# One decoder block on one core: orders of ACT's work, place of a weight load, banks and slots

## The chip, the cores and the metric

The kernel runs on 1 core of one Trainium2 chip. The metric is the device time of one execution in microseconds; the time before is the median of 3 runs.

## The reference

The block mixes 1024 tokens of width 1024 by two mixers and ends with a feed-forward layer, all in float32:

```python
u = rmsnorm(h, ln_mix);  z = u @ w_in        # columns: latents, GLA q/k/v/low rank/gate, gate_a, gate_b
y_a = mla(c_q, c_kv, k_rope, ...) @ mla_w_o  # 8 heads, causal; k_rope: one rotary key shared by the heads
y_b = gla(g_q, g_k, g_v, g_lr, ...) @ gla_w_o
#   log_a = log_sigmoid(g_lr @ w_gate2 + b_gate) / 16; chunked scan over the tokens with decay exp(cumsum(log_a))
h = h + (sigmoid(gate_a) * y_a + sigmoid(gate_b) * y_b) @ w_out
u = rmsnorm(h, ln_ffn)
h = h + (silu(u @ w_gate) * (u @ w_up)) @ w_down
out = rmsnorm(h, final_norm)
```

## The kernel before, in words

A float32 product is made of three TensorE matmuls: each operand is split into a rounded high part and a low part that holds the rest, and `mm3` (L132 to L134) adds high by high, high by low and low by high. The high part of a weight is a cast on ACT (L114, L160), the low part a subtraction on DVE or POOL (L115, L161). So each product of 128x128 by 128x512 has three matmuls, and each new weight block costs a DMA, a cast and a subtraction before them. Large products are cut into a 2x2 scheme with fewer block products (`pair`, `p_first`, `p_second` and so on), whose partial sums go through tiles `st`.

The program is written stage by stage; a scheduler then sets the order of the instructions on each engine from the written order, the dependencies and the slots of the pools. Every engine then works through its own list strictly in order, and SP issues nearly all loads and stores from one such list. Weights arrive in pool tag `wr` (4 slots of 128x1024); a load can only start when the last reader of its slot is done.

**Input (L303 to L335).** SP loads the gains `g_mix` (L92, through `gain_cols`), then four tiles of x. They are normalised (`norm_in`: square on ACT, `rx` on POOL, scaling on DVE), turned by PE into 8 PSUM banks (chunks c0 to c7, four of them with tag `ps_mm`), and each chunk is read three times: by ACT with the gain (L316, high part), by DVE (L317, low part) and by ACT again (L329, an unsplit copy `raw0`). `begin` then makes two blocks of q, from weights `wh`/`wl`. The first product writes a `ps_mm` bank, so it needs the first chunk's bank back.

**Log decay (L413 to L431).** Four half tiles go through Abs and Exp (L422, L423) and, in a second loop, through Ln (L430). The sums over the chunks follow on PE (L441).

**Gates and rotary key (L740 to L860).** Behind the scan come the latents' norms (`latents`, `token_rows`), the last two pairs of blocks of gate_b (`O_GB + 512`, `O_GB + 768`), the rotary key `krr` (L793 to L800: a load of 64x1024, a product with the table on DVE, two matmuls with `sel`), and `up_weights(1)`, which loads two 128x1024 pieces of w_ukv (L726) into `wr` and splits them (L728, L729).

**Feed-forward layer.** The second half of the tokens is turned in `second_half` (L1320 to L1347): eight transposed chunks, all in PSUM tag `B` (4 banks). Slots of 128x1024 come from pool `r4` (14).

**Down projection (L1380 to L1500).** The hidden activations come back from DRAM as `xr` (9 slots), the weights as `dr`/`y` (`load_y(c, 0)` and `load_y(c, 1)`). Loop b0 runs over 11 chunks (`chunk`: 12 matmuls, eight with the high, four with the low part of `xr`), then loop b1 with the difference of the two weight halves (L1500).

Of the kernel before, what the change touches and what calls it, by code (L numbers as in the profile page):

```python
# [10 lines left out]
F32 = mybir.dt.float32  # L11
# [9 lines left out]
P = 128  # L21
S = 1024
# [26 lines left out]
def block_kernel(ctx, tc, x, positions, ln_mix, w_in, norm_cq, w_uq, norm_ckv, w_ukv, w_oa,  # L49
# [29 lines left out]

    ident = const.tile([P, P], F32, name="ident")  # L80
# [8 lines left out]

    g_mix = gain_cols(ln_mix[0], KC, "g_mix")  # L90
# [179 lines left out]
    with ExitStack() as s1:  # L270
# [35 lines left out]
        def begin(off, out, e):  # L306
            w = wload(win[:, off:off + P], KC, P, nc.vector)
            out(e, 0, proj(w, 0), True)
            first.append((w, out, e))
# [5 lines left out]
        def turned_split(dst, ps, gc):  # L315
            nc.scalar.activation(dst[0], ps, AF.Copy, scale=gc)  # L316
            nc.vector.scalar_tensor_tensor(dst[1], ps, gc, dst[0].bitcast(F32), ALU.mult, ALU.subtract)  # L317

# [4 lines left out]
        xn = [norm_in(load_x(t)) for t in range(4)]  # L323
        for c in range(KC):
# [3 lines left out]
            turned_split(T[("B11", "B21")[j]][k], ps, gc)  # L328
            nc.scalar.activation(raw0[k][j], ps, AF.Copy, scale=gc)  # L329
        begin(O_GQ, out_q, 0)  # L330
        begin(O_GQ + P, out_q, 1)
# [83 lines left out]
    for i in range(4):  # L415
# [7 lines left out]
        nc.scalar.activation(ab, ab, AF.Exp, scale=-1.0)  # L423
# [5 lines left out]
    for ab, l in la:  # L429
        nc.scalar.activation(ab, ab, AF.Ln, bias=1.0)  # L430
# [352 lines left out]
    def q_split(c, half, cr):  # L783
# [20 lines left out]

# [48 lines left out]
    wv_h, wv_l = (t.rearrange("p (c h n) -> p c h n", c=2, h=8) for t in wtiles2())  # L853
    up_weights(1, wv_h, wv_l)
# [3 lines left out]
    p_second(w, out_gb)  # L858
    tab = [uslot(0, F32) for e in range(2)]
# [244 lines left out]
    def slot(name, dt=F32):  # L1104
        return r4.tile([P, S], dt, name=name, tag="r4", bufs=14)
# [50 lines left out]
    def transposed(xn, cc):  # L1156
        ps = pbank("B", 4)
# [162 lines left out]
    def second_half():  # L1320

        T = []
        for c in range(4):
# [6 lines left out]
            p22 = transposed(xn1, c + 4)  # L1330
# [237 lines left out]
```

## Time and profile before

| what | before |
|---|---|
| median of 3 runs | 1518.63 us (1518.12 to 1520.06) |
| the profiled execution's own time | 1514.89 us |
| its span | 1513.2 us |
| PE busy | 1456.1 us, 96% |
| DVE / ACT / POOL busy | 67% / 44% / 31% |
| mean granted clock of TensorE | 0.989 |

The profiled execution is 3.74 us below the median. Outside its span lie 1.7 us. PE is busy for 96% of the span, so about 57 us of idle PE are spread over it. A granted clock of 1.00 is 2.4 GHz, one of 0.50 is 1.2 GHz.

### The profile page before, as it was taken

Reading aid. Unit: us, or ns where it says so; the run is one execution under the profiler, and the core shown is the slowest. Engines: PE = TensorE matmul, PEld = TensorE weight load, DVE = VectorE, ACT = ScalarE, POOL = GpSimd, SP = SyncE. Lnnn points to the kernel's source line nnn. Section 1 sums busy time; section 2 is a strip of 40 time slices with the busy share of each in tenths; the row PEclk is TensorE's granted clock in tenths of the full one; section 3 lists DMA queues with packets and bytes.
Section 4 is the critical chain, followed back from the end, with each engine's and each line's share of the span. In section 5 each row is a group of like instructions: output and inputs, shape, how many; then the busy total and the mean of one; then the engine's idle time right before and its main releaser. Section 6 shows DMA issues by size and latency. Waiting matters only on the chain.

```text
span 1513.2 us, 20379 instructions
## 1 busy us (share of the span) xinstructions
PE 1456.1 (96%) x7454; PEld 1214.8 (80%) x7454; DVE 1017.8 (67%) x1459; ACT 673.3 (44%) x1329; POOL 464.0 (31%) x406
## 2 busy tenths in 40 slices
PE   6999999999979999999999899999999999899997
PEld 5789887788757888877899778888888888688886
DVE  4867886888474777574612876666666667876875
ACT  6553344644454766576302632222222223254454
POOL 1311230212102114234812455555555554100000
PEclk9999999999989999999999999999999999999999
DMA  7124234242431004258722223233223324943461
GB/s 228 46 91 151 84 104 133 63 132 92 139 105 51 9 35 139 99 168 269 263 81 84 84 71 98 97 105 105 98 98 105 101 94 166 399 131 95 135 195 56
DMA packets 123158, 181.52 MB, mean 120 GB/s; under 512 B 12897, under 2 KB 76914, under 8 KB 123058
## 3 DMA queue, kind: packets, MB, share of 16 engines
q1 hardware_dynamic: 122482, 178.38, 35.8%
q10 hardware_dynamic: 576, 1.84, 0.3%
q8 instruction: 59, 0.97, 0.3%
q14 instruction: 41, 0.34, 0.1%
HBM read 125.66 MB, written 54.53 MB: 119 GB/s over the span
## 4 chain that ended last, share of the span: by engine, by line
PE 49%; DVE 3%; DMA 1%; issue 0%; ACT 0%; POOL 0%; DVEq 0%; POOLq 0%
PE psB L133 6%; PE psB L134 6%; PE psB L132 6%; PE psA L132 4%; PE psA L134 4%; PE psD L134 4%; PE psD L132 4%; PE psD L133 4%; PE psA L133 4%; PE psy L134 1%; PE psy L132 1%; PE psy L133 1%; DMA xr<-d_a 1%; DMA dr<-in_ffn_w_down_dram 0%; DVE UT L161 0%; DMA d_h<-h 0%
## 5 line engine op out<-in xcount | busy, mean ns | idle before, releaser
L161 DVE TENSOR_TENSOR ws<-wr,ws 128x512 fp32r<-128x512 f32 x135 | 128.3, 960 | 15.5 <-ACT ws L160 14.9
L160 ACT CAST ws<-wr 128x512 fp32r<-128x512 f32 x157 | 94.2, 617 | 64.6 <-DVE wr L177 25.7
L95 POOL TENSOR_TENSOR rx<-rs_m,nhalf 128x1 f32<-128x1 f32 x24 | 14.8, 623 | 264.5 <-DVE rs_m L94 263.1
L132 PE MATMUL ps_mm<-u,ws 128*128 128x512 f32 x208 | 84.5, 407 | 10.9 <-ACT st L204 10.3
L161 POOL TENSOR_TENSOR ws<-sS,ws 128x512 fp32r<-128x512 f32 x44 | 70.7, 1616 | 67.9 <-ACT ws L160 67.9
L134 PE MATMUL ps_mm<-u,ws 128*128 128x512 f32 x208 | 83.3, 404 | 0.0
L133 PE MATMUL ps_mm<-u,ws 128*128 128x512 f32 x208 | 83.1, 399 | 0.0
L160 ACT CAST ws<-xr 128x512 fp32r<-128x512 f32 x73 | 45.2, 621 | 84.3 <-PE psB L134 39.1
L1206 ACT COPY p<-psA 128x512 f32<-128x512 f32 x22 | 12.9, 587 | 156.6 <-PE psA L134 156.6
L612 POOL TENSOR_TENSOR X<-E,gk 128x512 f32<-128x512 f32 x28 | 42.0, 1506 | 129.9 <-ACT E L610 69.7
L161 DVE TENSOR_TENSOR ws<-xr,ws 128x512 fp32r<-128x512 f32 x73 | 50.2, 688 | 37.1 <-ACT ws L160 34.5
L133 PE MATMUL psB<-UT,ws 128*128 128x512 f32 x176 | 69.8, 397 | 2.4 <-DVE UT L161 2.4
L176 DVE TENSOR_TENSOR st<-st,ps_mm 128x512 f32<-128x512 f32 x75 | 51.1, 683 | 30.9 <-PE ps_mm L134 28.8
L132 PE MATMUL psB<-UT,ws 128*128 128x512 f32 x176 | 69.8, 396 | 0.1
L132 PE MATMUL psA<-UB,ws 128*128 128x512 f32 x176 | 69.6, 396 | 0.0
L134 PE MATMUL psB<-UT,ws 128*128 128x512 f32 x176 | 69.6, 395 | 0.0
L134 PE MATMUL psA<-UB,ws 128*128 128x512 f32 x176 | 69.5, 395 | 0.0
L133 PE MATMUL psA<-UB,ws 128*128 128x512 f32 x176 | 69.3, 394 | 0.0
L935 DVE TENSOR_TENSOR ws<-pspt,ws 128x512 fp32r<-128x512 f32 (+1 forms) x80 | 49.6, 632 | 17.4 <-ACT ws L934 16.9
L916 ACT ACTIVATE u<-pss,nb 128x128 f32<-128x128 f32 (+3 forms) x64 | 47.8, 747 | 25.0 <-DVE nb L914 14.7
L160 ACT CAST ws<-sS 128x512 fp32r<-128x512 f32 x88 | 50.3, 619 | 18.1 <-DVE sS L1182 18.1
L132 PEld LDWEIGHTS ps_mm<-u,ws 128*128 128x128 f32 x208 | 39.4, 189 | 20.7 <-ACT st L204 10.8
(464 smaller groups left out, 4734.8 us busy)
## 6 DMA issues: line engine op xcount, KB each, us to landing
xr<-d_a SPq DMA_DIRECT2D x73, 256.0 KB, 2.9
wr<-in_w_in_dram SPq DMA_DIRECT2D x32, 512.0 KB, 4.1
wr<-in_ffn_w_gate_dram SPq DMA_DIRECT2D x22, 512.0 KB, 3.8
wr<-in_ffn_w_up_dram SPq DMA_DIRECT2D x22, 512.0 KB, 3.8
d_a<-p SPq DMA_DIRECT2D x20, 512.0 KB, 2.9
dr<-in_ffn_w_down_dram SPq DMA_DIRECT2D x14, 512.0 KB, 6.8
d_a<-R SPq DMA_DIRECT2D x10, 512.0 KB, 2.6
xt<-in_x_dram SPq DMA_DIRECT2D x8, 512.0 KB, 6.4
```

Of the source, the lines that this page charges most:

```text
L95: nc.gpsimd.tensor_tensor(dst, m, nhalf[:, :n], ALU.pow)
L132: nc.tensor.matmul(ps, ah, bh, start=first, stop=False, **kw)
L133: nc.tensor.matmul(ps, ah, bl, start=False, stop=False, **kw)
L134: nc.tensor.matmul(ps, al, bh, start=False, stop=last, **kw)
L160: nc.scalar.copy(dst[:, 0], src)
L161: (lo_eng or nc.gpsimd).tensor_tensor(dst[:, 1], src, dst[:, 0].bitcast(F32), ALU.subtract)
L176: plus = lambda d, x, y: nc.vector.tensor_tensor(d, x, y, ALU.add)
L612: nc.gpsimd.tensor_tensor(X, E, k, ALU.mult)
L916: nc.scalar.activation(pt[:, 0:w], ps[:, 0:w], AF.Exp, bias=bias, accum_out=sums[h // 2][:, t, e:e + 1])
L935: nc.vector.tensor_tensor(tl[:, 0:w], ps[:, 0:w], th[:, 0:w].bitcast(F32), ALU.subtract)
L1206: nc.scalar.copy(tt[:, 0:HALF], psA)
```

## The change

1. Input: `g_mix` is loaded behind the first four tiles of x. The second L316 (c1) is put behind the first chunk's copy. The low parts of the first two weights go to POOL.
2. Log decay: each Ln is put behind the last Exp that was written.
3. `O_GB + 768`'s loads and its `p_first` and `p_second` are written ahead of `krr` and of `up_weights(1)`.
4. Feed-forward layer: pool `r4` has 15 slots; the chunks `p22` of `second_half` are turned into PSUM tag `D` (2 banks).
5. Down projection: `xr` has 14 slots; `load_y(., 1)` starts at c = 8, no longer at c = 4.

`behind` adds an order on one engine, no semaphore.

```diff
@@ -77,6 +77,12 @@
     const = pool("const", side="left")
     wpool = pool("wpool", side="left")
 
+    def behind(later, first):
+
+        tc.add_manual_dep(later.ins, first.ins.name,
+                          mybir.DependencyInfo(mybir.DependencyClass.NoSync, mybir.DependencyReason.DATA),
+                          reason="issue order")
+
...
@@ -86,8 +92,6 @@
         t = const.tile([P, n], F32, name=name)
         nc.sync.dma_start(t, ap.rearrange("(c p) -> p c", p=P))
         return t
-
-    g_mix = gain_cols(ln_mix[0], KC, "g_mix")
 
     def rstd_of(dst, ssq, n, scale, epool):
         m = epool.tile([P, n], F32, name="rs_m", tag="rs_m")
@@ -303,8 +307,8 @@
                 mm3(ps, w[0][:, c, :], w[1][:, c, :], *T[f"B{j + 1}{half + 1}"][k], c == 0, c == KC - 1)
             return ps
 
-        def begin(off, out, e):
-            w = wload(win[:, off:off + P], KC, P, nc.vector)
+        def begin(off, out, e, lo_eng=nc.vector):
+            w = wload(win[:, off:off + P], KC, P, lo_eng)
             out(e, 0, proj(w, 0), True)
             first.append((w, out, e))
 
@@ -313,22 +317,28 @@
             minus(dst[1], src, dst[0].bitcast(F32))
 
         def turned_split(dst, ps, gc):
-            nc.scalar.activation(dst[0], ps, AF.Copy, scale=gc)
+            hi = nc.scalar.activation(dst[0], ps, AF.Copy, scale=gc)
             nc.vector.scalar_tensor_tensor(dst[1], ps, gc, dst[0].bitcast(F32), ALU.mult, ALU.subtract)
+            return hi
 
         out_q = store(d_q, (0, P), scale=0.125)
         out_k = store(d_k, (0, P))
 
         raw0 = [parts(v4(F32)) for c in range(4)]
-        xn = [norm_in(load_x(t)) for t in range(4)]
+        xs0 = [load_x(t) for t in range(4)]
+        g_mix = gain_cols(ln_mix[0], KC, "g_mix")
+        xn = [norm_in(xt) for xt in xs0]
+        copied = None
         for c in range(KC):
             j, k = divmod(c, 4)
             gc = g_mix[:, c:c + 1]
             ps = turned(xn, c, "mm" if c < 4 else "g")
-            turned_split(T[("B11", "B21")[j]][k], ps, gc)
-            nc.scalar.activation(raw0[k][j], ps, AF.Copy, scale=gc)
-        begin(O_GQ, out_q, 0)
-        begin(O_GQ + P, out_q, 1)
+            hi = turned_split(T[("B11", "B21")[j]][k], ps, gc)
+            if c == 1:
+                behind(hi, copied)
+            copied = nc.scalar.activation(raw0[k][j], ps, AF.Copy, scale=gc)
+        begin(O_GQ, out_q, 0, nc.gpsimd)
+        begin(O_GQ + P, out_q, 1, nc.gpsimd)
         xn = [norm_in(load_x(t)) for t in range(4, 8)]
         begin(O_GK, out_k, 0)
         t12, t4 = [], []
@@ -420,14 +430,14 @@
                              wg2[0:17, :], start=True, stop=True)
         ab = g.tile([P, HALF], F32, name="lab", tag=("E", "gk")[i // 2], bufs=2)
         nc.scalar.activation(ab, ps, AF.Abs)
-        nc.scalar.activation(ab, ab, AF.Exp, scale=-1.0)
+        ex = nc.scalar.activation(ab, ab, AF.Exp, scale=-1.0)
         if i % 2 == 0:
             la2 = g.tile([P, S], F32, name="la", tag="A", bufs=2)
         l = la2[:, (i % 2) * HALF:(i % 2 + 1) * HALF]
         nc.vector.tensor_scalar(l, ps, 0.0, None, ALU.min)
         la.append((ab, l))
     for ab, l in la:
-        nc.scalar.activation(ab, ab, AF.Ln, bias=1.0)
+        behind(nc.scalar.activation(ab, ab, AF.Ln, bias=1.0), ex)
         nc.vector.tensor_tensor(l, l, ab, ALU.subtract)
     def gb_tile():
         return g.tile([P, HALF], F32, name="gb", tag="gb", bufs=2)
@@ -789,19 +799,6 @@
     sc_q = small.tile([P, NT], F32, name="sc_q", tag="sc_q", bufs=1)
     nc.vector.tensor_scalar(sc_q, rs_q, 96.0 ** -0.5, None, ALU.mult)
     rq_ps = token_rows(sc_q)
-
-    krr = wraw(1024)[0:64]
-    nc.sync.dma_start(krr, d_c[640:704, :])
-    nc.vector.tensor_tensor(krr, krr, rot[0:64], ALU.mult)
-    nc.gpsimd.tensor_tensor(sel, ident[0:64, 0:32].unsqueeze(1).broadcast_to([64, 4, 32]),
-                            ident[0:64, 32:64].unsqueeze(1).broadcast_to([64, 4, 32]), ALU.add)
-    kr_ps = []
-    for half in range(2):
-        ps = bank("g")
-        nc.tensor.matmul(ps, sel.rearrange("p a b -> p (a b)"), krr[:, half * HALF:(half + 1) * HALF],
-                         start=True, stop=True)
-        kr_ps.append(ps)
-
     pair(columns(O_GB + 512), store(d_gb, (512, 640), AF.Sigmoid))
 
 
@@ -850,12 +847,25 @@
         return q[:, 0, :], q[:, 1, :]
 
 
-    wv_h, wv_l = (t.rearrange("p (c h n) -> p c h n", c=2, h=8) for t in wtiles2())
-    up_weights(1, wv_h, wv_l)
     w = weights(columns(O_GB + 768))
     out_gb = store(d_gb, (768, 896), AF.Sigmoid)
     p_first(w)
     p_second(w, out_gb)
+
+    krr = wraw(1024)[0:64]
+    nc.sync.dma_start(krr, d_c[640:704, :])
+    nc.vector.tensor_tensor(krr, krr, rot[0:64], ALU.mult)
+    nc.gpsimd.tensor_tensor(sel, ident[0:64, 0:32].unsqueeze(1).broadcast_to([64, 4, 32]),
+                            ident[0:64, 32:64].unsqueeze(1).broadcast_to([64, 4, 32]), ALU.add)
+    kr_ps = []
+    for half in range(2):
+        ps = bank("g")
+        nc.tensor.matmul(ps, sel.rearrange("p a b -> p (a b)"), krr[:, half * HALF:(half + 1) * HALF],
+                         start=True, stop=True)
+        kr_ps.append(ps)
+
+    wv_h, wv_l = (t.rearrange("p (c h n) -> p c h n", c=2, h=8) for t in wtiles2())
+    up_weights(1, wv_h, wv_l)
     tab = [uslot(0, F32) for e in range(2)]
     Kh[0], Kl[0] = ([uslot(0) for e in range(2)] for x in "hl")
     for half in range(2):
@@ -1102,7 +1112,7 @@
     r4 = pool("r4", side="right", c=hx)
 
     def slot(name, dt=F32):
-        return r4.tile([P, S], dt, name=name, tag="r4", bufs=14)
+        return r4.tile([P, S], dt, name=name, tag="r4", bufs=15)
 
     h_tm = [slot(f"h{t}") for t in range(NT)]
     for t in range(NT):
@@ -1153,8 +1163,8 @@
             nc.vector.tensor_scalar(xt, xt, r, None, ALU.mult)
         return xn
 
-    def transposed(xn, cc):
-        ps = pbank("B", 4)
+    def transposed(xn, cc, tag="B"):
+        ps = pbank(tag, 2 if tag == "D" else 4)
         for i in range(4):
             nc.tensor.transpose(ps[:, i * P:(i + 1) * P], xn[i][:, cc * P:(cc + 1) * P], ident)
         return ps
@@ -1327,7 +1337,7 @@
             T.append((T1, T2))
             p12 = transposed(xn1, c)
             nc.vector.scalar_tensor_tensor(T1, p12, g0, raw0[c][:, 0:HALF], ALU.mult, ALU.subtract)
-            p22 = transposed(xn1, c + 4)
+            p22 = transposed(xn1, c + 4, "D")
             nc.vector.scalar_tensor_tensor(T2, p22, g1, T1, ALU.mult, ALU.subtract)
             b22 = U["B22"][c]
             nc.scalar.activation(b22[:, 0], p22, AF.Copy, scale=g1)
@@ -1384,7 +1394,7 @@
                 x_first.append(slot("xf"))
             t = x_first[-1][:, (c % 2) * HALF:(c % 2 + 1) * HALF]
         else:
-            t = dp.tile([P, HALF], F32, name="xr", tag="xr", bufs=9)
+            t = dp.tile([P, HALF], F32, name="xr", tag="xr", bufs=14)
         ordered_load(t, d_a[c][i][:, k * HALF:(k + 1) * HALF])
         return t
 
@@ -1470,8 +1480,8 @@
             load_y(c + IN_R4, 0)
         if c == 1:
             pair_out(NPAIR - 1, st)
-        if c >= 4:
-            load_y(c - 4, 1)
+        if c >= 8:
+            load_y(c - 8, 1)
         chunk(b0, c, "11", Y[c][0])
     E11, V5, U2, U3 = (acc(nm) for nm in ("E11", "V5", "U2", "U3"))
     for t in range(4):
@@ -1479,8 +1489,8 @@
 
     b1 = newbanks(1)
     for c in range(NC):
-        if c + NC - 4 < NC:
-            load_y(c + NC - 4, 1)
+        if c + NC - 8 < NC:
+            load_y(c + NC - 8, 1)
         nc.vector.tensor_tensor(Y[c][0], Y[c][1], Y[c][0], ALU.subtract)
         chunk(b1, c, "S1", Y[c][0])
     fn_b = dp.tile([P, D], F32, name="fn_b")
```

ACT at the input, from the casts of the first two weights; u0 is the high part of a chunk, v4 its copy. Before, then with the change:

```order
L114 CAST wh_227<-wr_229 128x1024
L114 CAST wh_261<-wr_263 128x1024
L316 ACTIVATE u0_97<-ps_mm_163,g_mix_80 128x512
L316 ACTIVATE u0_98<-ps_mm_171,g_mix_80 128x512
L316 ACTIVATE u0_99<-ps_mm_179,g_mix_80 128x512
L316 ACTIVATE u0_100<-ps_mm_187,g_mix_80 128x512
L316 ACTIVATE u0_101<-ps_g_195,g_mix_80 128x512
L316 ACTIVATE u0_102<-ps_g_203,g_mix_80 128x512
L316 ACTIVATE u0_103<-ps_g_211,g_mix_80 128x512
L316 ACTIVATE u0_104<-ps_g_219,g_mix_80 128x512
L329 ACTIVATE v4_119<-ps_mm_163,g_mix_80 128x512
L329 ACTIVATE v4_120<-ps_mm_171,g_mix_80 128x512
```

```order
L118 CAST wh_227<-wr_229 128x1024
L118 CAST wh_261<-wr_263 128x1024
L320 ACTIVATE u0_95<-ps_mm_163,g_mix_129 128x512
L339 ACTIVATE v4_117<-ps_mm_163,g_mix_129 128x512
L320 ACTIVATE u0_96<-ps_mm_171,g_mix_129 128x512
L320 ACTIVATE u0_97<-ps_mm_179,g_mix_129 128x512
L320 ACTIVATE u0_98<-ps_mm_187,g_mix_129 128x512
L320 ACTIVATE u0_99<-ps_g_195,g_mix_129 128x512
L320 ACTIVATE u0_100<-ps_g_203,g_mix_129 128x512
L320 ACTIVATE u0_101<-ps_g_211,g_mix_129 128x512
L320 ACTIVATE u0_102<-ps_g_219,g_mix_129 128x512
L339 ACTIVATE v4_118<-ps_mm_171,g_mix_129 128x512
```

The copy of the first chunk (bank ps_mm_163) moves from behind eight gain reads to behind one; the other copies stay behind the eighth.

ACT at the last gate pairs. Before, wr_3879 and wr_3880 are the loads of `O_GB + 768` and wh_3869 is w_ukv; with the change those are wr_3861 and wr_3862, and wh_3909 is w_ukv. The copy to st_3753 (st_3745) empties the bank that `p_second` of `O_GB + 512` writes next:

```order
L160 CAST ws_3833<-wr_3734 128x512
L784 ACTIVATE c2_3658<-wc_3673,g_cq_3607 128x512
L728 CAST wh_3869<-wr_3871 128x512
L728 CAST wh_3869<-wr_3875 128x512
L784 ACTIVATE c2_3659<-wc_3669,g_cq_3607 128x512
L784 ACTIVATE c2_3660<-wc_3671,g_cq_3607 128x512
L784 ACTIVATE c2_3661<-wc_3673,g_cq_3607 128x512
L160 CAST ws_3884<-wr_3879 128x512
L160 CAST ws_3901<-wr_3880 128x512
L204 COPY st_3753<-ps_mm_3737 128x512
L160 CAST ws_3944<-wr_3879 128x512
L266 ACTIVATE st_3789<-ps_mm_3737 128x512
```

```order
L164 CAST ws_3825<-wr_3726 128x512
L794 ACTIVATE c2_3658<-wc_3673,g_cq_3607 128x512
L164 CAST ws_3866<-wr_3861 128x512
L794 ACTIVATE c2_3659<-wc_3669,g_cq_3607 128x512
L794 ACTIVATE c2_3660<-wc_3671,g_cq_3607 128x512
L164 CAST ws_3883<-wr_3862 128x512
L794 ACTIVATE c2_3661<-wc_3673,g_cq_3607 128x512
L738 CAST wh_3909<-wr_3911 128x512
L164 CAST ws_3944<-wr_3861 128x512
L208 COPY st_3745<-ps_mm_3729 128x512
L738 CAST wh_3909<-wr_3915 128x512
L270 ACTIVATE st_3781<-ps_mm_3729 128x512
```

The two casts of gate weights that stood directly ahead of the copy have moved up between the L794 rows. A cast of w_ukv (L738) and the next gate cast (L164, ws_3944) now stand directly ahead of the copy instead.

ACT at the start of the down projection; xr_11523 (xr_11521) is chunk 4's `xr`, xr_11547 (xr_11543) chunk 5's, y80 the weight of chunk 8:

```order
L160 CAST ws_11528<-dr_11429 128x512
L160 CAST ws_11552<-y50_11431 128x512
L160 CAST ws_11574<-y60_11451 128x512
L160 CAST ws_11596<-y70_11479 128x512
L160 CAST ws_11525<-xr_11523 128x512
L160 CAST ws_11618<-y80_11499 128x512
L160 CAST ws_11549<-xr_11547 128x512
L160 CAST ws_11571<-xr_11569 128x512
L160 CAST ws_11593<-xr_11591 128x512
```

```order
L164 CAST ws_11526<-dr_11429 128x512
L164 CAST ws_11548<-y50_11431 128x512
L164 CAST ws_11568<-y60_11451 128x512
L164 CAST ws_11588<-y70_11479 128x512
L164 CAST ws_11523<-xr_11521 128x512
L164 CAST ws_11545<-xr_11543 128x512
L164 CAST ws_11610<-y80_11499 128x512
L164 CAST ws_11565<-xr_11563 128x512
L164 CAST ws_11632<-y90_11519 128x512
L164 CAST ws_11585<-xr_11583 128x512
```

The cast of chunk 5's `xr` moves ahead of the cast of y80. On SP, the loads of the `xr` of chunks 5, 6 and 7 stood behind one piece of `load_y(., 1)` each, and now stand ahead of the first such piece.

## Rows read from the trace of the kernel before

**Rows 1.** The page: busy time, share of the span and instructions of each engine.
```profile
PE 1456.1 (96%) x7454; PEld 1214.8 (80%) x7454; DVE 1017.8 (67%) x1459; ACT 673.3 (44%) x1329; POOL 464.0 (31%) x406
```

**Rows 2.** Timeline, PE, 19 to 26 us: start, duration, engine, line; in brackets idle before, releaser.
```profile
19.28 0.79 PE L132 MATMUL ps_mm<-u,wh 128*128 128x512 f32 x1 [5.48 <-ACT v L329]
25.40 0.40 PE L134 MATMUL ps_mm<-u,wl 128*128 128x512 f32 x1
25.63 0.40 PE L132 MATMUL ps_mm<-u,wh 128*128 128x512 f32 x1
```

**Rows 3.** Timeline, ACT, 12 to 19 us.
```profile
13.92 2.42 ACT L316 ACTIVATE u<-ps_mm,g_mix 128x512 fp32r<-128x512 f32 x4
18.49 0.74 ACT L329 ACTIVATE v<-ps_mm,g_mix 128x512 f32<-128x512 f32 x1
```

**Rows 4.** Stretches: each engine's busy us, then granted clock, DMA share, GB/s.
```profile
18.00:19.00 1.00, 0.00 (x0) 0.00 (x0) 1.00 (x2) 1.00 (x3) 0.00 (x0) 0.77 1.16 294
866.00:872.00 6.00, 4.45 (x20) 3.30 (x19) 6.00 (x8) 1.24 (x2) 1.89 (x2) 1.00 0.00 0
1305.00:1307.00 2.00, 0.77 (x3) 0.56 (x3) 1.19 (x2) 1.38 (x3) 0.00 (x0) 0.59 1.05 420
```

**Rows 5.** Lines by form: one line's groups; durations in ns, least/median/most, then starts.
```profile
L115 POOL TENSOR_TENSOR wl<-wr,wh x8: 2397/2404/2857, 720.9 to 798.6; 128x1024 fp32r<-128x1024 f32 x8
L115 DVE TENSOR_TENSOR wl<-wr,wh x4: 1219/1225/1226, 12.6 to 25.2; 128x1024 fp32r<-128x1024 f32 x4
```

**Rows 6.** Timeline, ACT, 96 to 107 us (first and last of five table loads), PE at 109.
```profile
97.24 1.28 ACT L430 ACT_TABLE_LOAD   x1
106.50 1.28 ACT L430 ACT_TABLE_LOAD   x1
...
109.30 1.13 PE L441 MATMUL ps_g<-tri,la 128*128 128x128 f32 x8 [1.36 <-DVE la L431]
```

**Rows 7.** Timeline, PE, ACT, DVE and SP's queue, 423 to 432 us.
```profile
431.92 0.79 PE L132 MATMUL ps_mm<-u,ws 128*128 128x512 f32 x1 [9.58 <-ACT st L204]
...
430.76 0.62 ACT L160 CAST ws<-wr 128x512 fp32r<-128x512 f32 x1 [2.67 <-DMA wr<-in_w_in_dram]
431.29 0.58 ACT L204 COPY st<-ps_mm 128x512 f32<-128x512 f32 x1
...
423.07 0.68 DVE L161 TENSOR_TENSOR ws<-wr,ws 128x512 fp32r<-128x512 f32 x1
425.62 2.06 DVE L785 SCALAR_TENSOR_TENSOR c<-wc,g_cq,c 128x512 fp32r<-128x512 f32 x3
...
423.78 1.64 SPq L182 DMA_DIRECT2D wr<-in_w_in_dram  x2
```

**Rows 8.** DMA issues: out<-in, xcount, KB each, median us from issue to landing.
```profile
wr<-in_mla_w_ukv_dram SPq DMA_DIRECT2D x4, 512.0 KB, 3.8
```

**Rows 9.** Timeline, PE, at 869 us (feed-forward layer) and at 232 us (scan).
```profile
869.09 0.50 PE L133 MATMUL psB<-UT,ws 128*128 128x512 f32 x1 [1.55 <-DVE UT L161]
...
231.87 0.70 PE L663 MATMUL ps_g<-gv,kdT 128*128 128x256 f32 x2 [1.60 <-ACT kdT L648]
```

**Rows 10.** Timeline, PE, 1299 to 1312 us: start of the down projection.
```profile
1299.87 0.50 PE L132 MATMUL psA<-ws 128*128 128x512 f32 x1 [1.28 <-ACT ws L160]
1303.92 0.73 PE L134 MATMUL psA<-ws 128*128 128x512 f32 x2 [1.94 <-DVE ws L161]
1306.35 0.79 PE L132 MATMUL psA<-ws 128*128 128x512 f32 x1 [1.23 <-ACT ws L160]
1311.63 0.63 PE L132 MATMUL psA<-ws 128*128 128x512 f32 x1
```

**Rows 11.** Timeline, SP's queue and ACT, 1296 to 1306 us.
```profile
1297.15 0.81 SPq L1120 DMA_DIRECT2D xr<-d_a  x1
...
1305.16 0.62 ACT L160 CAST ws<-y 128x512 fp32r<-128x512 f32 x1 [5.34 <-PE psD L134]
1305.68 0.61 ACT L160 CAST ws<-xr 128x512 fp32r<-128x512 f32 x1
```

## The prediction, made before the changed kernel was timed

> **What bounds the kernel now.** I read the page first, then PE's waits, then at each large wait the timeline of the engine that ended it. PE is busy for 96% of the span [rows 1], and the chain that ended last is PE nearly throughout. So only two things can be won: idle time of PE, and time in which PE runs at half clock. The large idle times are few: 5.48 us at the input [rows 2], 1.36 at the log decay [rows 6], 9.58 at the last gate pairs [rows 7], and 1.28, 1.94 and 1.23 at the start of the down projection [rows 10]. Behind three of them the granted clock falls: it is 0.77 in the stretch from 18 to 19 us and 0.59 from 1305 to 1307 us [rows 4], on its way from 1.00 (2.4 GHz) to 0.50 (1.2 GHz). At half clock, matmuls of 512 columns start 0.44 us apart (14 of them from 19.28 to 25.40), at full clock 0.23 apart (25.40 to 25.63) [rows 2].
>
> **Input.** PE turns the first chunks until 13.80 (19.28 less 5.48) and then waits for ACT's first copy, which frees the bank of its first product [rows 2, 3]. ACT makes eight gain reads first, at 0.6 us each from 13.92, so the copy starts at 18.49 [rows 3]. With the change it is second: gain read to 14.5, copy to 15.2, PE starts at about 15.2, 4.1 us earlier. The low parts go to POOL: 2.40 us instead of 1.22 for such a tile [rows 5]. DVE made the first from 12.6 on [rows 5]; POOL then has them at about 15.0 and 17.4. The first is wanted by the third matmul at 15.7, so the slower engine is hidden; with a start 1 us later it would cost 0.3 us. `g_mix` behind the loads of x costs nothing that I see: ACT reads it only at 13.92.
>
> The next wait is then the second product's bank, freed by the copy of c1, which stands behind the gain read of c7: 13.92 + 9 x 0.6 + 0.7 = 20.0. Of the first product 19 of 24 matmuls stand ahead of that wait, and the gain reads deliver them by 18.7, so PE idles for about 1.1 us there. An idle of 1.4 us and one of 1.1 us are near the 1.55 us at 869.09 [rows 9], in a stretch with the clock at 1.00 [rows 4]; the fall at the input came 5 us into an idle of 5.48. I therefore take full clock. By 25.40 PE had started 14 matmuls; now 19, and 5.4 / 0.23 = 23 more: 42. The 28 are worth 28 x 0.23 = **6.5 us**. Bounds: 3.0 (4.1 less 1.1, clock falls after all) and 6.8 (4.1 and 14 x 0.2, no second wait).
>
> **Log decay.** Ahead of the last Ln, ACT has five table loads of 1.28 us, from 97.24 to 106.50, because the scheduler mixes Exp and Ln [rows 6]. With the change one load is left there: 4 x 1.28 = 5.1 us less of ACT. PE had other products to do meanwhile and waited only 1.36 us for the last difference [rows 6]. I take **1.4 us**; bounds 0 and 1.4. The Trainium skill, page "ScalarE: Activation LUTs", section "Table sets: the hidden batching unit", says that one set holds both exp and ln, so that using them together costs one load; by that rule there would be nothing to save here, and the sum would be 12.4 instead of 13.8. The trace shows a load at nearly every change between the two, so the measurement decides.
>
> **Last gate pairs.** The code moves `O_GB + 768` ahead of `krr` and `up_weights(1)`, so its two weight loads no longer wait for a slot until 423.78 [rows 7]. Those loads held the casts at 430.76, and the copy at 431.29 behind them held PE until 431.92 [rows 7]. It seems that 9.58 us go. They do not, by the order of ACT: directly ahead of the same copy now stand a cast of w_ukv (L738) and the next gate cast. W_ukv's load inherits the slot that freed at 423.75, the end of DVE's subtraction from 423.07 [rows 7]. And the product of `krr` has moved into DVE's list ahead of that subtraction: a tile of 1024 columns, 1.2 us by the 1.22 of another such subtraction on DVE [rows 5]. So: slot free at 424.95, issue at 425.0, landing 3.8 later [rows 8] at 428.8, cast 0.62 to 429.4. The gate cast behind it waits for DVE to make a sum of the two weights, seven larger instructions behind the subtraction: 7 x 0.69 (three of L785 take 2.06 [rows 7]) = 4.8, to 429.75. Cast to 430.4, copy (0.58) to 430.9, PE at 430.9 instead of 431.92: **1.0 us**. The clock falls there as before. Bounds: 0 and 2. The later loads of w_ukv now follow one another through one slot, each 3.8 + 0.62 + 0.68 = 5.1 us; the products with the first two pieces come about 30 us behind the wait (some 100 matmuls of gate_b lie between), so 10 us of loading are hidden. If that cover were gone, it would be the 10 us.
>
> **Feed-forward layer.** PE's wait of 1.55 us is for DVE [rows 9], and DVE is busy for all 6.00 us of that stretch [rows 4]. More banks let PE turn chunks earlier, but DVE has the same instructions to do. I take **0**; bounds 1.6 either way (the wait goes, or comes once more). The slot of `r4` I cost at nothing: PE has no wait worth naming from there to the down projection.
>
> **Scan.** The scheduler also mixes the loops of the scan anew. Between the hand-offs of the recurrence (L656, L663) PE still has 20 to 25 other matmuls, as before, by the order; its longest wait there is 1.60 [rows 9]. I take 0, bounds 1.6 either way.
>
> **Down projection.** The first wait (1.28) ends with ACT's queue and stays. The second (1.94, to 1303.92) is for the low part of chunk 4's `xr` [rows 10]; on DVE two instructions of 0.6 us no longer stand ahead of it: 1.2 us less. The third (1.23) is for the cast of chunk 5's `xr` at 1305.68, which stands behind a cast that waits 5.34 us for PE to free a buffer [rows 10, 11]. In the new order it stands ahead of that cast. Its data was issued at 1297.15 [rows 11], half a w_ukv piece and so there by 1301: the 1.23 go. After idles of 1.28 and 0.7 I expect full clock; chunk 5's 12 matmuls from 1306.35 to 1311.63 [rows 10] then take 12 x 0.23 = 2.8 instead of 5.28, another 2.5. Sum **4.9 us**; bounds 2.4 (half clock as now) and 6.2 (the first wait goes too).
>
> **Sum.** 6.5 + 1.4 + 1.0 + 4.9 = 13.8 us. Against the profiled execution's own 1514.89 this is 1501.1; that execution lies 3.74 below the median, and on the median the forecast is **1504.8 us**.
>
> **Rivals.**
> - The wait at the last gate pairs goes. For it: the late weight loads now come early. Against: the two casts ahead of the copy. Worth 9.58 and 12 matmuls at full instead of half pace, 2.5: 12.1 instead of 1.0, so 1493.7. Chance 0.12. It decides if w_ukv's load finds a slot some 9 us sooner than I hold.
> - The clock falls at the input and the down projection all the same, and the log decay gives nothing: 3.0 + 1.0 + 2.4 = 6.4, so 1512.2. For it: shorter idles remain in both places. Against: the 1.55 at 1.00. Chance 0.18.
> - ACT changes tables as often as now, so that the change does not do what it says at the log decay: 12.4, so 1506.2. Against: one load stands in the new order. Chance 0.04. The rule that the Trainium skill states (page "ScalarE: Activation LUTs", above) would end at this time too.
> - All terms at their low ends: 1.8 us of gain, 1516.8, no change that can be told. Chance 0.07.
> - Slower: the scan. It has 12 hand-offs (three for each of 4 heads). If the new mix leaves each a wait like today's longest, 1.60 [rows 9], PE loses 19.2 and the whole is 5.4 slower: 1524.0. It decides from 1.4 us at each, (13.8 + 3.0) / 12. Against: the number of matmuls between hand-offs is the same. Chance 0.07.
>
> **Numbers.** A measurement of this kernel can tell about 0.2%, 3.0 us. The forecast has a chance of 0.52, with 1500 to 1510 as its own range. Faster is 0.52 + 0.12 + 0.18 + 0.04 = 0.86; no change 0.07; slower 0.07. The range from 1493 to 1513 takes in the first three rivals and leaves out 0.14.
>
> **What would show it.** Input: PE's first product near 15.2, a granted clock of 1.00 from 15 to 26 us, a wait of about 1 us before the second product. Log decay: one table load before the Ln. Gate pairs: still a wait of 8 to 9 us, ended by ACT's copy (L208), with half clock behind it; if it is under 2 us, my step on the order is wrong. Down projection: no wait of 1.23 before chunk 5, and a clock of 1.00 there. New waits of over 1 us in the scan would make the sum wrong.

## The result and the profile after

The changed kernel takes 1501.59 us (median of 4 runs, 1499.67 to 1505.29), the kernel before 1518.38 in its 4 runs of the same comparison: ratio 0.9891, 95% interval 0.987 to 0.9913, so 1.1% faster. The forecast was 1504.8, from 1493 to 1513. The profiled execution took 1499.67 us, its span is 1497.8 and its mean granted clock 0.991.

The page's first part, after, answers to [rows 1]:

```profile
PE 1452.3 (97%) x7454; PEld 1214.1 (81%) x7454; DVE 1014.8 (68%) x1457; ACT 665.8 (44%) x1323; POOL 474.2 (32%) x408
```

PE's busy time falls by only 3.8 us of the 15.4 by which the span falls; the rest was idle time. Where the gain lies is read from four points of PE's timeline, in both traces: a, the first matmul of the log decay's product (17 partitions); b, the last sum of the latents' squares (L755 before, L765 after); c, the matmul that ends the first wait of the down projection; d, the end.

| stretch | before | after | less |
|---|---|---|---|
| start to a (input) | 94.3 | 89.8 | 4.5 |
| a to b (log decay, scan) | 327.8 | 324.1 | 3.7 |
| b to c (gate pairs, attention, feed-forward) | 877.8 | 875.9 | 1.9 |
| c to d (down projection) | 213.3 | 208.0 | 5.3 |

Lines of the changed kernel stand 4 to 10 higher: L132 is L136, L160 is L164, L204 is L208, L316 is L320, L329 is L339, L441 is L451.

**Input.** The timelines of PE, ACT and POOL after, against [rows 2, 3, 5]:

```profile
15.94 0.79 PE L136 MATMUL ps_mm<-u,wh 128*128 128x512 f32 x1 [2.35 <-ACT v L339]
16.52 0.63 PE L137 MATMUL ps_mm<-u,wh 128*128 128x512 f32 x1
...
19.44 0.39 PE L138 MATMUL ps_mm<-u,wl 128*128 128x512 f32 x1
19.67 0.40 PE L136 MATMUL ps_mm<-u,wh 128*128 128x512 f32 x1
```
```profile
13.70 0.67 ACT L320 ACTIVATE u<-ps_mm,g_mix 128x512 fp32r<-128x512 f32 x1
15.20 0.69 ACT L339 ACTIVATE v<-ps_mm,g_mix 128x512 f32<-128x512 f32 x1 [0.82 <-DVE u L321]
```
```profile
12.01 4.67 POOL L119 TENSOR_TENSOR wl<-wr,wh 128x1024 fp32r<-128x1024 f32 x2 [1.01 <-ACT wh L118]
```

The copy is second on ACT now, as the order said, and PE starts 3.3 us earlier. But the copy waits 0.82 us for DVE's subtraction (L321), which reads the same bank. And the clock falls. Here are the stretches that this section uses, those of later stages too (busy us of PE, its weight loads, DVE, ACT and POOL, then granted clock, DMA share, GB/s), against [rows 4]:

```profile
15.00:18.00 3.00, 2.06 (x5) 1.68 (x6) 1.67 (x4) 2.81 (x5) 2.60 (x3) 0.66 1.05 381
18.00:20.00 2.00, 2.00 (x8) 1.58 (x7) 2.00 (x4) 2.00 (x5) 0.00 (x0) 0.66 1.16 290
20.00:23.00 3.00, 3.00 (x15) 2.41 (x14) 1.19 (x2) 3.00 (x6) 0.00 (x0) 1.00 0.84 124
415.00:420.00 5.00, 0.00 (x0) 0.00 (x0) 5.00 (x10) 1.01 (x2) 1.92 (x1) 0.53 0.33 105
420.00:425.00 5.00, 2.56 (x6) 2.09 (x7) 3.46 (x7) 1.72 (x3) 2.70 (x1) 0.50 0.09 12
852.00:858.00 6.00, 5.91 (x22) 4.39 (x22) 6.00 (x9) 2.33 (x5) 2.96 (x2) 0.72 0.00 0
1290.00:1295.00 5.00, 4.24 (x18) 3.15 (x18) 4.25 (x8) 1.72 (x3) 0.00 (x0) 1.00 1.04 367
1295.00:1300.00 5.00, 5.00 (x24) 4.13 (x23) 4.04 (x7) 1.81 (x5) 0.00 (x0) 1.00 0.98 356
```

**Log decay.** ACT's timeline after, against [rows 6]: one table load, then the four Ln; and PE goes into the cumulative sums (L451) with no wait.

```profile
95.47 1.28 ACT L440 ACT_TABLE_LOAD   x1
96.76 2.19 ACT L440 ACTIVATE lab<-lab 128x512 f32<-128x512 f32 x4
```
```profile
99.28 3.73 PE L451 MATMUL ps_g<-tri,la 128*128 128x128 f32 x32
```

**Last gate pairs.** PE, ACT, DVE and SP's queue after, against [rows 7]:

```profile
422.44 0.80 PE L136 MATMUL ps_mm<-u,ws 128*128 128x512 f32 x1 [8.32 <-ACT st L208]
...
420.17 0.62 ACT L738 CAST wh<-wr 128x512 fp32r<-128x512 f32 x1 [4.16 <-DMA wr<-in_mla_w_ukv_dram]
421.28 0.62 ACT L164 CAST ws<-wr 128x512 fp32r<-128x512 f32 x1 [0.49 <-DVE wr L181]
421.81 0.58 ACT L208 COPY st<-ps_mm 128x512 f32<-128x512 f32 x1
...
412.93 1.21 DVE L857 TENSOR_TENSOR wr<-wr,rot 64x1024 f32<-64x1024 f32 x1
415.99 0.67 DVE L165 TENSOR_TENSOR ws<-wr,ws 128x512 fp32r<-128x512 f32 x1
...
416.69 7.20 SPq L736 DMA_DIRECT2D wr<-in_mla_w_ukv_dram  x2
```

The large wait is still there, 8.32 us in place of 9.58, ended by the same copy. DVE's subtraction frees w_ukv's slot, the load is issued at 416.69, ACT waits for it, and the copy stands two casts behind.

**Down projection.** PE's timeline after, against [rows 10]: two waits instead of three, and the piece that began at half clock before (12 matmuls, 5.28 us) runs from 1293.70 to 1296.45.

```profile
1289.79 0.50 PE L136 MATMUL psA<-ws 128*128 128x512 f32 x1 [1.30 <-ACT ws L164]
1292.65 0.74 PE L138 MATMUL psA<-ws 128*128 128x512 f32 x2 [0.76 <-DVE ws L165]
1293.70 0.40 PE L136 MATMUL psA<-ws 128*128 128x512 f32 x1
1296.45 0.39 PE L136 MATMUL psA<-ws 128*128 128x512 f32 x1
```

**Feed-forward layer.** PE's three longest waits after come to 4.19 us. Before they were 1.55 [rows 9], 0.81 and 1.63, together 3.99, each ended by DVE; two of them now end with ACT:

```profile
851.91 0.56 PE L136 MATMUL psB<-UT,ws 128*128 128x512 f32 x1 [1.91 <-ACT UT L164]
860.21 0.50 PE L136 MATMUL psB<-UT,ws 128*128 128x512 f32 x1 [1.11 <-ACT UT L164]
869.37 0.50 PE L136 MATMUL psD<-UB,ws 128*128 128x512 f32 x1 [1.17 <-DVE R L1243]
```

The granted clock falls here now (0.72 from 852 to 858 us). In all ten traces of kernels with the change or most of it, it is at half for some 3.5 us somewhere between 845 and 877 us; in the three traces without the change it is at no time half there. By those 3.5 us at half pace that is an estimated 1.7 us lost.

**Scan.** PE's waits there, grouped by line (total, times, longest), from 100 to 335 us: none that comes back at each hand-off.

```profile
PE ps_g L630 <- POOL X L622: 2.6, 2, 1.4
PE ps_g L673 <- ACT kdT L658: 1.7, 1, 1.7
```

### The profile page after: what moved, and what is told of

Its sections match the earlier page's. It is cut to its first block, busy times and chain, and to the rows that moved or that the text cites. A ratio compares the mean times of both kernels' runs of the same rounds, so it can differ in the third digit from the quotient of the medians.

```text
span 1497.8 us, 20362 instructions
## 1 busy us (share of the span) xinstructions
PE 1452.3 (97%) x7454; PEld 1214.1 (81%) x7454; DVE 1014.8 (68%) x1457; ACT 665.8 (44%) x1323; POOL 474.2 (32%) x408
## 3 DMA queue, kind: packets, MB, share of 16 engines
q10 hardware_dynamic: 576, 1.84, 0.3%
## 4 chain that ended last, share of the span: by engine, by line
PE 50%; DVE 3%; POOL 0%; ACT 0%; issue 0%; DMA 0%; DVEq 0%; ACTq 0%; POOLq 0%
PE psB L137 6%; PE psB L136 6%; PE psB L138 6%; PE psD L138 5%; PE psD L136 5%; PE psD L137 5%; PE psA L138 5%; PE psA L136 5%; PE psA L137 5%; PE psy L138 1%; PE psy L136 1%; PE psy L137 1%; DVE UT L165 0%; DVE h L1163 0%; PE psB L1169 0%
## 5 line engine op out<-in xcount | busy, mean ns | idle before, releaser
L165 DVE TENSOR_TENSOR ws<-wr,ws 128x512 fp32r<-128x512 f32 x135 | 131.4, 983 | 18.9 <-ACT ws L164 18.4
L164 ACT CAST ws<-wr 128x512 fp32r<-128x512 f32 x157 | 94.3, 618 | 76.6 <-DVE wr L181 33.3
L99 POOL TENSOR_TENSOR rx<-rs_m,nhalf 128x1 f32<-128x1 f32 x24 | 14.7, 619 | 252.1 <-DVE rs_m L98 250.7
L136 PE MATMUL ps_mm<-u,ws 128*128 128x512 f32 x208 | 83.9, 405 | 9.0 <-ACT st L208 9.0
L164 ACT CAST ws<-xr 128x512 fp32r<-128x512 f32 x73 | 45.1, 620 | 77.3 <-PE psD L138 35.0
L136 PE MATMUL psB<-UT,ws 128*128 128x512 f32 x176 | 70.0, 397 | 3.4 <-ACT UT L164 3.4
L136 PE MATMUL psA<-UB,ws 128*128 128x512 f32 x176 | 69.7, 396 | 0.0
L164 ACT CAST ws<-sS 128x512 fp32r<-128x512 f32 x88 | 50.3, 619 | 18.1 <-DVE sS L1192 18.1
L924 DVE TENSOR_REDUCE nb<-pss 128x1 f32<-128x128 f32 (+3 forms) x64 | 47.9, 752 | 12.2 <-PE pss L922 11.9
```

The source lines that it names most:

```text
L99: nc.gpsimd.tensor_tensor(dst, m, nhalf[:, :n], ALU.pow)
L136: nc.tensor.matmul(ps, ah, bh, start=first, stop=False, **kw)
L164: nc.scalar.copy(dst[:, 0], src)
L165: (lo_eng or nc.gpsimd).tensor_tensor(dst[:, 1], src, dst[:, 0].bitcast(F32), ALU.subtract)
L924: nc.vector.tensor_reduce(bias, ps[:, 0:w], AX.X, ALU.max, negate=True)
```

## The experiments

Ratios below are to the kernel before, run beside each on the same chip, with 95% intervals. A kernel that differs little from the changed one (the one with DVE's low parts, whose local change is at most 0.7 us) came out at 0.9908, against 0.9891 for the changed one: some 2.6 us of 1518 between comparisons mean nothing here. So each part is judged by the stretches of the table above, and by the ratio only where it moves more. The stretch from b to c scatters too, from 875.9 to 879.3 among kernels with nothing changed in it.

**One part undone at a time.** The input (the loads' order, the place of the second gain read, the low parts):

```diff
+    g_mix = gain_cols(ln_mix[0], KC, "g_mix")
...
-            if c == 1:
-                behind(hi, copied)
...
-        begin(O_GQ, out_q, 0, nc.gpsimd)
-        begin(O_GQ + P, out_q, 1, nc.gpsimd)
+        begin(O_GQ, out_q, 0)
+        begin(O_GQ + P, out_q, 1)
```

> The changed kernel with the input as it was (gains first, eight gain reads ahead of the copies, low parts on DVE). My theory: the input is a gain of its own that later stages keep, 4.5 us by the start of the first low-rank decay matmul in the two traces, so the time is 1506.1 and the whole later profile is shifted by 4.5 us. The rival, that part of it is caught up in a later wait (as on a load), expects less, 1502 to 1504.

Measured: 1503.62 us, 0.9914 (0.99 to 0.9929). The wait of before is back, and point a stands at 93.0; in nine kernels with the new order it stands at 88.8 to 91.7. The part is worth 1.3 to 4.2 us, by the clock that follows. Nothing of it is caught up later, as the rival has it: this trace is 3.2 us behind the changed kernel's at a and 3.4 at b.

```profile
19.34 0.80 PE L138 MATMUL ps_mm<-u,wh 128*128 128x512 f32 x1 [5.38 <-ACT v L337]
```

The low parts alone, on DVE again:

```diff
-        begin(O_GQ, out_q, 0, nc.gpsimd)
-        begin(O_GQ + P, out_q, 1, nc.gpsimd)
+        begin(O_GQ, out_q, 0)
+        begin(O_GQ + P, out_q, 1)
```

> The changed kernel with the first two low parts on DVE again, ACT's order kept. My theory: DVE's part of the first chunk stands behind two low parts of 1.2 us and ACT's copy waits for that part, so PE starts near 16.9 in place of 15.9 to 16.2 and the clock falls for longer: 1 to 2 us, 1502.6 to 1503.6. The rival, that ACT's order alone makes the gain, expects PE at 16.0 and 1501.6.

Measured: 1502.93 us, 0.9908 (0.9888 to 0.9928); PE starts at 16.60, against 15.94 to 16.48 in kernels with POOL. The copy begins at 15.86 there, just behind DVE's subtraction of the same chunk, which ends at 15.82; so the copy follows that subtraction here too. ACT's order makes the gain, together with the loads' new place; POOL adds 0.1 to 0.7 us. The place of the `g_mix` load was not undone by itself: with it the first transposes begin at 7.41 us instead of 8.27, but the last ones at 12.99 instead of 13.20.

The log decay:

```diff
-        behind(nc.scalar.activation(ab, ab, AF.Ln, bias=1.0), ex)
+        nc.scalar.activation(ab, ab, AF.Ln, bias=1.0)
```

> The changed kernel with Ln free to stand among the Exp again. My theory: five table loads come back on ACT, PE waits 1.4 us for the last difference again and runs longer at half clock, so the stretch to the scan is about 2.5 us longer, 1504.1. The rival, that the scan's new order gives the gain, expects that the waits of the scan change too and the time moves by 3.5 us or more, 1505. If only ACT were relieved it would be 1501.6.

Measured: 1508.97 us, 0.9947 (0.9931 to 0.9963). From a to b it is 330.0 us against 324.1: 5.9, four times my term (by the two ratios it would be 8.5, with the scatter named above). PE's timeline shows why:

```profile
99.75 1.16 PE L451 MATMUL ps_g<-tri,la 128*128 128x128 f32 x8 [1.60 <-DVE la L441]
103.73 3.56 PE L451 MATMUL ps_g<-tri,la 128*128 128x128 f32 x16 [2.82 <-DVE la L441]
```

The two waits come to 4.4 us where the kernel before shows 1.36. The kernel before, in the same place, has a clock of 0.63 and 0.52:

```profile
96.00:100.00 4.00, 4.00 (x15) 3.00 (x14) 2.18 (x4) 3.92 (x7) 0.00 (x0) 0.63 0.45 130
100.00:104.00 4.00, 4.00 (x21) 4.00 (x20) 1.18 (x2) 3.96 (x6) 0.00 (x0) 0.52 0.00 0
```

There PE did its other products at half clock and so came late to the wait. The chain on ACT, not PE, set when the sums could go on; the slow clock had hidden most of that. A further kernel below (the one before with `token_rows` moved) has the order of Exp and Ln of before and a clock of 1.00 in both stretches; its waits there are 1.51 and 2.70:

```profile
96.00:100.00 4.00, 4.00 (x29) 3.51 (x28) 2.29 (x4) 3.95 (x6) 0.00 (x0) 1.00 0.37 119
100.00:104.00 4.00, 3.39 (x30) 3.18 (x28) 0.76 (x2) 3.96 (x6) 0.00 (x0) 1.00 0.00 0
104.90 1.16 PE L441 MATMUL ps_g<-tri,la 128*128 128x128 f32 x8 [1.51 <-DVE la L431]
108.88 1.50 PE L441 MATMUL ps_g<-tri,la 128*128 128x128 f32 x8 [2.70 <-DVE la L431]
```

To see this part by itself, the kernel before with the order of the Ln alone (and the helper `behind`):

```diff
-        nc.scalar.activation(ab, ab, AF.Exp, scale=-1.0)
+        ex = nc.scalar.activation(ab, ab, AF.Exp, scale=-1.0)
...
-        nc.scalar.activation(ab, ab, AF.Ln, bias=1.0)
+        behind(nc.scalar.activation(ab, ab, AF.Ln, bias=1.0), ex)
```

> The kernel before with the order of Ln behind the last Exp, nothing else of the change. My theory: the prediction sized this term by the one wait of 1.4 us, but undoing it in the changed kernel cost 5.5 us between the first decay matmul and the latents' sums; so done alone it should bring 4 to 5.5 us: 1512 to 1513 by a median of 1516.8 for the kernel before. The rival, that the term is 1.4 us in the old order of PE and 5.5 only beside the other parts, expects 1515.4.

Measured: 1513.88 us, median of 8 runs, 0.9987 (0.997 to 1.0003). Its trace has no wait at the sums, a clock of 1.00 from 96 to 104 us, and 322.9 us from a to b, 4.9 less than before:

```profile
103.45 3.73 PE L447 MATMUL ps_g<-tri,la 128*128 128x128 f32 x32
```

These 4.9 are not the order's alone. The wait that is gone gives 1.4; the rest is the half clock of the kernel before from 97 to 104 us, about 3.5 (7 us at half pace). That this fall belongs to the order of the Ln is not shown: with the old order and `token_rows` moved, the clock is 1.00 there too. So by the traces the order is worth 1.4 us where PE comes to the sums at half clock, as before, and the waits of 4.2 to 4.4 us where it comes at nearly full clock. The timing, 2.0 us with an interval from 4.5 of gain to none, can't tell the two apart.

The last gate weights (`krr` and `up_weights(1)` ahead of `O_GB + 768` again):

```diff
     rq_ps = token_rows(sc_q)
+    krr = wraw(1024)[0:64]
...
+    up_weights(1, wv_h, wv_l)
     w = weights(columns(O_GB + 768))
```

> The changed kernel, but the rotary key and the w_ukv pieces are again written ahead of the last gate pair. My theory: the move only exchanged one wait for another, so its undoing costs 1 to 1.5 us (9.5 us of wait instead of 8.3): 1502.6 to 1503.1 by the median of the changed kernel, 1501.59. The rival, that the move is worth more because it also spares loads and DVE's time in the scan, expects 3 us or more: 1504.6 and up. In the trace PE's wait on ACT's copy is 9.5 us and the scan's waits are those of the changed kernel.

Measured: 1503.83 us, 0.9919 (0.9904 to 0.9935). The wait is 9.20 instead of 8.32, and from b to its end 9.5 us instead of 8.6: the part is worth 0.9 us there, close to what was worked out.

```profile
424.90 0.79 PE L136 MATMUL ps_mm<-u,ws 128*128 128x512 f32 x1 [9.20 <-ACT st L208]
```

The feed-forward layer (14 slots, the chunks in tag `B` again):

```diff
-        return r4.tile([P, S], dt, name=name, tag="r4", bufs=15)
+        return r4.tile([P, S], dt, name=name, tag="r4", bufs=14)
...
-            p22 = transposed(xn1, c + 4, "D")
+            p22 = transposed(xn1, c + 4)
```

> The changed kernel with 14 slots and all transposed chunks in one tag. My theory: DVE bounds that stretch, so the time from the first transposes to the first gate products of the layer moves by less than 1 us: 1501.6, within 1. The rival, that the banks hold PE, expects the waits of 1.6 and 0.8 us of the kernel before to come back on top of today's: 2 us or more, 1503.6.

Measured: 1504.32 us, 0.9914 (0.9895 to 0.9932). Its three longest waits are all on DVE, 1.56, 0.81 and 1.62, in place of 1.91, 1.11 and 1.17: 3.99 us against 4.19. From b to c it is 878.5, within the scatter, and its time lies 2.7 us above the changed kernel's, about what comparisons scatter by. The half clock is there without the part too, from 872.6 to 876.0 us. The part can't be told from nothing.

The down projection (9 slots, the second half's sums from c = 4 again):

```diff
-            t = dp.tile([P, HALF], F32, name="xr", tag="xr", bufs=14)
+            t = dp.tile([P, HALF], F32, name="xr", tag="xr", bufs=9)
...
-        if c >= 8:
-            load_y(c - 8, 1)
+        if c >= 4:
+            load_y(c - 4, 1)
```

> The changed kernel with 9 slots of xr and the second weight halves from chunk 4 on. My theory: the waits of 1.9 and 1.2 us and the half clock behind them come back, 5.3 us, 1506.9, and nothing ahead of the down projection moves. The rival, that the earlier waits set the clock there, expects the half clock gone all the same: 2.4 us, 1504.0.

Measured: 1508.3 us, 0.9938 (0.9919 to 0.9957). The three waits are back, half clock behind the last (0.50 from 1302 to 1304), and c to d is 212.2 us against 207.9 to 208.5 in every kernel that has the part: 3.6 to 4.2. How much of it is the clock shows in the kernel before with `token_rows` moved: it has the old code and waits of 1.28, 1.84 and 1.23, but no half clock behind them, and takes 210.7 us, 2.2 to 2.8 more than with the part. The slots and the later loads were not undone apart.

```profile
1299.11 0.73 PE L138 MATMUL psA<-ws 128*128 128x512 f32 x2 [1.93 <-DVE ws L165]
1301.53 0.80 PE L136 MATMUL psA<-ws 128*128 128x512 f32 x1 [1.23 <-ACT ws L164]
```

**Can the wait of 8 us go?** The theory says that the two casts ahead of the copy hold it. So both are put behind an earlier copy, that of `O_GB + 512`, with the same kind of order as the change uses:

```diff
-            nc.scalar.copy(hi[:, c], r4_)
+            cast = nc.scalar.copy(hi[:, c], r4_)
+            if first:
+                behind(cast, first)
...
-    up_weights(1, wv_h, wv_l)
+    up_weights(1, wv_h, wv_l, w5["copy"])
```

> The changed kernel with the cast of w_ukv and the next gate cast put behind the copy that frees the bank of p_second (an order on ACT alone). My theory: these two casts hold PE for 8.3 us. Without them ahead of it the copy runs when ACT is done with the gains of the latents, near 416 in place of 421.8 us, and PE's wait falls to about 2.5 us; 12 matmuls later PE then waits for the rows of the latents' norm, which DVE has near 425, so that only about 3 us are won in all: 1498.6 by a median of 1501.59 for the changed kernel. The rival, that the copy itself is late by its data or slot, leaves the wait at 8.3 and the time at 1501.6.

Measured: 1503.71 us, 0.9908 (0.9891 to 0.9925). The copy runs at 416.39, and the wait falls to 2.42; the next one, for the diagonal tile of `token_rows`, is 2.23. Yet hardly any time is won: from b to the last matmul with `sel` it is 15.8 us against 16.1. The waits are short, but the clock falls at the first and once more behind the second:

```profile
417.01 0.79 PE L136 MATMUL ps_mm<-u,ws 128*128 128x512 f32 x1 [2.42 <-ACT st L210]
424.71 2.73 PE L782 MATMUL ps_g<-st,ones 128*128 128x512 f32 x4 [2.23 <-DVE st L779]
417.00:420.00 3.00, 2.99 (x7) 2.41 (x8) 3.00 (x7) 0.00 (x0) 1.45 (x1) 0.50 0.62 168
...
426.00:429.00 3.00, 3.00 (x4) 0.83 (x3) 2.86 (x5) 0.62 (x1) 0.00 (x0) 0.50 0.46 81
```

My reading is that PE has too little work between the last sum of squares and what hangs on it. Part of that is POOL: the reciprocal root (L99) on which the diagonal tile hangs took 4.61 us there, from 418.56, and DVE sat idle for the last 1.53 of it; in the kernel before it took 2.02. The three lines of `token_rows(sc_q)` ask for two `st` tiles that need that sum, and stand ahead of the gate pairs. With them written behind the last gate pair, ahead of `krr`, and both orders kept:

```diff
-    sc_q = small.tile([P, NT], F32, name="sc_q", tag="sc_q", bufs=1)
-    nc.vector.tensor_scalar(sc_q, rs_q, 96.0 ** -0.5, None, ALU.mult)
-    rq_ps = token_rows(sc_q)
...
     p_second(w, out_gb)
 
+    sc_q = small.tile([P, NT], F32, name="sc_q", tag="sc_q", bufs=1)
+    nc.vector.tensor_scalar(sc_q, rs_q, 96.0 ** -0.5, None, ALU.mult)
+    rq_ps = token_rows(sc_q)
```

> As x_copy_first, and the rows of the latents' norm (token_rows of cq) are written ahead of the rotary key, behind the last gate pair. My theory: with the copy early and these rows out of the way PE has its gate products all the time, the wait of 8.3 us falls to 2 or 3 us in all and the half clock behind it goes: 7 to 9 us, 1493 to 1495. The rival, that DVE bounds this stretch (it is busy for all of the wait), expects that new waits for DVE take the place: not below 1498.

Measured: 1494.79 us, 0.9856 (0.9833 to 0.988). Then the move alone, without the two orders (the diff just above, on the changed kernel):

> The changed kernel with the rows of the latents' norm written behind the last gate pair, without the two orders of x_copy_first. My theory: the ring of st slots is the whole cause, so the two orders add nothing, and this is as fast as x_rows_later: a ratio of 0.984 to 0.988 to the kernel before. The rival, that both are needed, expects the ratio of x_copy_first, 0.991.

Measured: 1494.61 us (1493.46 to 1495.26), 0.9854 (0.9839 to 0.9868): the orders add nothing. The interval lies wholly below the changed kernel's, so this one, and by its median the run before it, is faster than the change itself. PE and ACT there:

```profile
419.57 0.50 PE L136 MATMUL ps_mm<-u,ws 128*128 128x512 f32 x1 [0.83 <-ACT ws L164]
423.75 0.49 PE L138 MATMUL ps_mm<-u,ws 128*128 128x512 f32 x1 [1.11 <-DVE ws L165]
```
```profile
409.99 0.58 ACT L208 COPY st<-ps_mm 128x512 f32<-128x512 f32 x1
417.29 0.60 ACT L270 ACTIVATE st<-ps_mm 128x512 f32<-128x512 f32 x1 [1.04 <-PE ps_mm L138]
```

The copy now runs at 409.99, among the squares of the latents, long before PE wants its tile; the granted clock is 1.00 in all four stretches of 5 us from 405 to 425. Last, the same move in the kernel before, by itself:

```diff
-    sc_q = small.tile([P, NT], F32, name="sc_q", tag="sc_q", bufs=1)
-    nc.vector.tensor_scalar(sc_q, rs_q, 96.0 ** -0.5, None, ALU.mult)
-    rq_ps = token_rows(sc_q)
...
     pair(columns(O_GB + 512), store(d_gb, (512, 640), AF.Sigmoid))
+    sc_q = small.tile([P, NT], F32, name="sc_q", tag="sc_q", bufs=1)
+    nc.vector.tensor_scalar(sc_q, rs_q, 96.0 ** -0.5, None, ALU.mult)
+    rq_ps = token_rows(sc_q)
```

> The kernel before with one thing moved: the rows of the latents' norm (token_rows of cq) are written behind the pair O_GB + 512, no longer ahead of it. My theory: two tiles of these rows stand ahead of p_first's copy in the ring of five st slots, and it is this ring that makes the copy late; with them behind it, the 9.6 us of wait fall to 2 to 4 us although the last gate weights still load late: 1508 to 1511 by a median of 1516.8. The rival, that the late loads of the last gate weights hold PE in the kernel before, as the change supposes, expects the wait to move to the first product with these weights and not more than 3 us won: 1514 or more.

Measured: 1504.65 us, 0.992 (0.9902 to 0.9938). PE has no wait for that copy (it runs at 416.91), though the last gate weights still come late: ACT waits 2.29 us for them at 430.40. From a to c it is 1196.1 us, 9.5 less than before. So the late weights, which the change moves, hold PE only where the copy stands behind their casts on ACT, as it did in the kernel before; with the copy ahead of them the same late weights cost PE no wait.

```profile
416.91 0.57 ACT L204 COPY st<-ps_mm 128x512 f32<-128x512 f32 x1
...
430.40 0.62 ACT L160 CAST ws<-wr 128x512 fp32r<-128x512 f32 x1 [2.29 <-DMA wr<-in_w_in_dram]
```

That the order of the `st` slots (5 of them, given out in the order of the program) ties the copy to the two tiles is the likely reason; the runs show only that the written order does it.

## Why the prediction was right, and where its terms were not

- **Input: predicted 6.5, measured 4.5.** Two steps failed. "Copy to 15.2" left out DVE's subtraction, which reads the same bank and for which the copy waits by the trace: it began at 15.20 instead of 14.5, so PE started 0.74 late. And "I therefore take full clock" was wrong: the idle was 2.35 us and no longer 1.4, and 8 matmuls ran 0.43 apart instead of 0.23, 1.6 us. The second product's wait of 1.1 us did not come, since PE got there later. About 34 matmuls had started by 25.40, not 42; 20 more than the 14 of before, at 0.23, are 4.6. The 4.5 lies inside the bounds of 3.0 to 6.8 (whose upper end, 4.1 and 14 x 0.2, is 6.9), and other pairs of kernels, with the old order and the new, give 1.3 to 5.6.
- **Log decay: predicted 1.4, measured 3.7 in the two traces for the whole stretch, 5.9 by undoing the part and 4.9 by doing it alone.** The mechanism was right, one load left and no wait; the term was mis-sized, and its upper bound too. The step that failed is "I take 1.4 us": it priced the wait as the trace showed it [rows 6], when PE came to that wait behind 7 us at half clock, a fall that the prediction did not see. At nearly full clock the waits there are 4.2 to 4.4 us. Of the 4.9 by doing it alone, about 3.5 are that half clock, which is not shown to be the order's; so what the part gave in this change lies between 1.4 and 5.9, and stays open there. By the Trainium skill (page "ScalarE: Activation LUTs", section "Table sets: the hidden batching unit") one set serves exp and ln and nothing was to be won; the traces before and after, with five loads and one ahead of the last Ln, do not agree with that.
- **Last gate pairs: predicted 1.0, measured 1.3 from b to the end of the wait.** Every link held. Counted from b, 8.2 us earlier than before, the forecast's slot, load, casts and copy fall at 416.8, 420.6, 421.6 and 422.2 for what was seen at 416.69, 420.17, 421.28 and 421.81. The rival in which the wait goes fell.
- **Feed-forward and scan: predicted 0.** No change of the time there can be told from nothing, though the clock now falls once in the feed-forward layer, where the prediction had it at 1.00; the scan's longest wait is 1.7, at one hand-off, so the slower rival fell.
- **Down projection: predicted 4.9, measured 5.3** by the two traces, 3.6 to 4.2 by undoing it, 2.2 to 2.8 where the old code ran without half clock. The first wait stayed (1.30), the second shrank by 1.18 where 1.2 was worked out (what is left of it is DVE's own list, through which it works without a gap up to that subtraction at 1291.91), the third went, and the clock stayed at 1.00. In two other kernels with the part, those with the gates or the feed-forward layer undone, it fell to half for some 3.5 us there, and c to d was 208.5 all the same.

The sum was 13.8, and the spans differ by 15.4. That agreement owes something to luck: the input's 2.0 too much and the log decay's 2.3 too little cancel, and several terms move by 2 us or more with where the clock happens to fall. In the rival with all terms at their low ends, 5.4 less twice 1.6 is 2.2, not 1.8. The rival with the clock falling at both places was half right, at the input; but there it lost 1.6 us, and it held nothing of the log decay's gain.

## What to carry to other kernels

A wait is priced with the clock that PE had on its way to it: work at half clock hides the other engine's lateness, and when the clock is mended upstream the wait grows unless that engine is mended too. When a large wait ends with one instruction, look at what stands ahead of that instruction on its engine and why, before making its neighbours' loads earlier; here three lines moved in the written order took away a wait that the moved loads had only shortened. And cutting one wait of 8 us into two of 2 won next to nothing here, because half clock came with each.

## What the runs showed of the hardware

- The same idle did not always cost the clock. At the input, nine kernels with the new order idle for 2.31 to 3.27 us; in eight the granted clock fell to half for some time up to 23 us, in one, after 3.06 us, it stayed at 1.00 (the one with the log decay undone). At the down projection, it fell behind waits of 1.28, 1.94 and 1.23 before; in the kernel before with `token_rows` moved it did not, behind 1.28, 1.84 and 1.23, and c to d took 210.7 us instead of 213.3. And at the log decay it fell from 97 to 104 us before, and PE had no wait there after 74 us. What decides it stays open.
- The same reciprocal root of 128x8 on POOL (L99, L95 before) took 2.02 us before and 4.61 after. DVE was busy all through the 2.02 and for the first 3.1 of the 4.61, so a busy DVE alone does not make the difference; the cause stays open. After, it held no wait of PE; with the copy first, PE's second wait hung on it.
